# An attention kernel's DMA queue in source order, shift rows two heads at a time, an earlier PSUM release, and one bank for each output half at the end

## The chip, the cores and the metric

The kernel runs on one core of one Trainium2 chip. The metric is the device time of one execution in microseconds (us), as the median of several runs. A core has five engines that run their own instruction streams and meet at semaphores: TensorE (PE, matmuls, with its weight loads shown as PEld), VectorE (DVE), ScalarE (ACT), GpSimd (POOL) and SyncE (SP), which here issues every DMA.

## The reference

One layer of a bidirectional encoder, run on a prompt of 1024 tokens and a sample of 2048 tokens with the same weights. Per layer and sequence:

```python
h = rms_norm(x, norm_pre)
z = h @ w_in        # split into u_pool, g_pool, q, k, v, g_attn, q_x, g_x
pool_out = multiscale_pool(u_pool) * silu(g_pool)
attn_out = block_self_attention(rope(rms_norm(q)), rope(rms_norm(k)), v) * silu(g_attn)   # 8 heads, 2 kv heads
x_out = memory_attention(q_x, k_m, v_m) * silu(g_x)      # 4 heads, 256 memory tokens
mix = concatenate([pool_out, attn_out, x_out])           # 1024 wide
y = mix @ w_out
return x + rms_norm(y, norm_post)
```

Everything is float32 in and out.

## The kernel before

**Two phases.** The first computes the projections, block by block, and puts q, k, v, the gates and the pooled channels into DRAM scratch. The second, which the change is about, does attention, the output projection and the final norm. It is written by hand as a list of *turns* (172 of them), and the loop at L954 to L981 emits one turn after another.

**Pairs, groups and turns.** A `Pair` is 256 query tokens; there are 8 pairs of the sample (s=1), then 4 of the prompt (s=0). Each pair has three `Group`s: kind 0 and kind 1 are the two kv heads of the self-attention (four query heads each), kind 2 is the memory attention. A group's keys come in chunks of 128, two chunks a turn, so a group of kind 0 or 1 takes 8 turns for the sample and 4 for the prompt, and a group of kind 2 one turn. The first pair runs kinds 2, 0, 1 (turns 0; 1 to 8; 9 to 16), every other pair 0, 2, 1.

**What a turn does.** Two *looks* (L171, `largest`): score matmuls into the PSUM tile `N` and a DVE reduction that takes the largest score of each query (L191); they work ahead for a group that comes later. When a group's last look is done, `shift` (L195) transposes the maxima on DVE (L127) and eight small DMAs lay them out as two rows of the tile `rows0` or `rows1` (L206). `weights` (L209) starts a chunk's scores in a PSUM tile `S` with a matmul that adds those rows (L216), adds the scores (L224), and ACT takes the exponential into an SBUF tile `P` (L226; five buffers). `sums` (L228) adds up the `P`s into `z`: for the sample one half of the columns on POOL (L238) and the other on DVE (L239), for the prompt all on DVE. `values` (L241) multiplies by V on PE (L251), each turn or every second turn.

**After a group.** `totals` (L255) sums `z` across partitions on PE, into the PSUM tile `acc`, or into `py` for kind 2 and for the first pair (L260). `take`, `turned` and `inverse` gate the result, transpose the totals, invert them, and send them through a DRAM scratch to be spread over 64 partitions: one DMA out (L280, `rows<-gz`) and two back (L283, `gz<-rows`; `gz` has one buffer). `mix_out` multiplies gate and inverse (L293) and splits the product in a high and a low part (L296, L300), on POOL except for the last pair.

**Output.** `Output.piece` (L366) does the output projection of 128 tokens in two halves of 512 columns, eight chunks of three matmuls each (L381 to L383), into the one PSUM bank `py`; for the last pair both halves share one tile `S` of two banks (`self.both`). `square` (L384) takes the sum of squares on ACT (L388), `scale` (L391) multiplies by the gain on DVE and so ends the use of the bank (L400), `norm` and `out` finish on POOL, ACT and DVE and store (L418). `project` (L934) hands out pieces in the turns without `values`: 4 pieces a turn in the sample, 8 in the prompt.

**What sets the order.** `at(turn, f)` files a step under a time such as turn + 1.4; `due` runs what is filed. Inside a turn the times are: loads and `.0`, first look, `.1`, `sums`, `.2`, weights, second look, `sums`, `.4`, `project`, `values` and `totals`, `.6`. PE, ACT, DVE and POOL follow this order in their streams, since the engines in the set `order` (L508) are under the manual schedule. SP is not in the set: its DMAs are placed by a scheduler that plays the program through with estimated times. On every engine the instructions run in stream order, so a DMA that waits for a semaphore on SP holds up all DMAs behind it.

**Loads at the start of the second phase.** `w_out` comes in eight chunks of 512 KB (L114, `raw<-w_out`), one every two turns, into two buffers; each is split by ACT and POOL in two steps (L118, L119), one a turn, in turns 3 to 18. K and V of a group are loaded when they are first asked for: V from `load_late`, the two other parts of K (DH, DL) from `shift`.

Of the kernel before, what the change touches and what calls it, by code (L numbers as in the profile page):

```python
# [7 lines left out]
F32 = mybir.dt.float32  # L8
# [15 lines left out]
def encoder(ctx, tc, I, O):  # L24
# [63 lines left out]
    has_K, has_V = set(), set()  # L88
# [13 lines left out]
    def load_V(s, kind):  # L102
        has_V.add((s, kind))
# [28 lines left out]
    class Group:  # L132
# [62 lines left out]
        def shift(self):  # L195

            if self.parts > 1:
                nc.vector.tensor_reduce(out=self.top[:, 0:8], in_=self.nb.rearrange("p a i -> p i a"),
                                        axis=AX.X, op=ALU.min)
                load_K(self.s, self.kind, DH, 1)  # L200
                load_K(self.s, self.kind, DL, 2)
            r = lanes_to_rows(self.top, "top")
            for j in range(2):
                row = self.rows[64 * j:64 * j + 1].rearrange("o (i b r) -> o i b r", b=4, r=32)
                for b in range(4):
                    nc.sync.dma_start(out=row[:, :, b].bitcast(F32), in_=r[32 * b + 4 * j:32 * b + 4 * j + 4])  # L206
# [65 lines left out]
        def inverse(self):  # L272
# [6 lines left out]
            rows = dram.tile([4, 256], F32, name="rows", tag="rows", bufs=4)  # L279
            nc.sync.dma_start(out=rows, in_=back[0:128:32])  # L280
            for j in range(2):
                src = rows[2 * j:2 * j + 2].rearrange("l q -> (l q)").unsqueeze(0)
# [65 lines left out]
    class Output:  # L348


        def __init__(self, pair, x):
            self.pair, self.x, self.last = pair, x, pair.last
            self.s, self.t = pair.s, 2 * pair.p + x
            self.both = None
# [11 lines left out]
        def piece(self, h, c, first, final):  # L366
            if self.last:
                if self.both is None:
                    self.start()
                    self.ss = dbl.tile([128, 2], F32, name="ssy", tag="ssy")  # L370
                    self.both = pss.tile([128, 1024], F32, name="S", tag="S")
                ps = self.both[:, 512 * h:512 * h + 512]
            else:
                if first:
                    if h == 0:
                        self.ss = dbl.tile([128, 2], F32, name="ssy", tag="ssy")
                    self.ps = pso.tile([128, 512], F32, name="py", tag="py")
                ps = self.ps
# [6 lines left out]
        def square(self, h):  # L385
            junk = own.tile([128, 512], mybir.dt.bfloat16, name="junk2", tag="junk2")
            src = self.both[:, 512 * h:512 * h + 512] if self.last else self.ps
            nc.scalar.activation(out=junk, in_=src, func=AF.Square, scale=D ** -0.5,  # L388
                                 accum_out=self.ss[:, h:h + 1])

        def scale(self, h):  # L391
            if h == 0 and not self.last:
                for m in sorted(later):
                    for x in [x for x in later[m] if x[0].__name__ in ("norm", "out")]:
                        later[m].remove(x)
                        x[0](*x[1])
                self.start()
            c = slice(512 * h, 512 * h + 512)
            src = self.both[:, c] if self.last else self.ps
            nc.vector.tensor_tensor(out=self.y[:, c], in0=src, in1=npost[:, c], op=ALU.mult)  # L400
# [8 lines left out]
        def out(self, h):  # L409
            s, t, x, y = self.s, self.t, self.xr, self.y  # L410
# [4 lines left out]
            else:  # L415
                nc.scalar.activation(out=y[:, c], in_=y[:, c], func=AF.Copy, scale=self.r[:, 0:1])
                nc.gpsimd.tensor_tensor(out=x[:, c], in0=x[:, c], in1=y[:, c], op=ALU.add)  # L417
            nc.sync.dma_start(out=O[("y_prompt", "y_sample")[s]][0, 128 * t:128 * t + 128, c],  # L418
                              in_=x[:, c])
# [36 lines left out]
    for pair in pairs:  # L456
# [5 lines left out]
        for g in pair.groups:  # L462
            wait = first[g] + g.chunks // 2 + (2 if pair.last else 3)
            at(wait + 0.6, g.mix_out, wait + 1, pair)
        at(max(ends) + (3 if pair.last else 7), open_fill, pair)
    value_runs, sums_at = {}, {}
    for g in groups:
# [4 lines left out]
        while k < c:  # L472
            run = 1 if n + k < first[pairs[1].groups[0]] + 6 else 2
# [550 lines left out]
```

## Time and profile before

| what | us |
|---|---|
| median of 3 runs | 1768.66 |
| lowest and highest run | 1767.05, 1769.37 |
| the profiled execution, its own time | 1766.64 |
| span of the trace in it | 1764.8 |
| of the span, PE busy | 1701.8 |
| DVE busy | 1102.5 |
| POOL busy | 840.2 |
| ACT busy | 657.0 |

In the trace the times count from the start of the span. The first phase ends on PE at about 710, the turns of the sample run to about 1490, those of the prompt to about 1710, and the output projection of the last two pairs ends the kernel. A PE that counts as busy may run at half its clock; the granted clock is shown beside it.

### The profile page before, as it was taken

The page shows a single profiled execution, that of the slowest core. Times are in us where ns is not written, and L with a number is a line of the kernel's source. Part 1 is how long each engine was busy: PE and PEld are TensorE (multiplying, and loading weights), DVE is VectorE, ACT ScalarE, POOL GpSimd, SP SyncE. Part 2 cuts the span into 40 slices and gives each one's busy share as a digit, 9 for nine tenths or more (in the row PEclk, how much of TensorE's full clock was granted, in tenths as well). Part 3 has the DMA queues.
Part 4 walks back from the last instruction along what each step waited for, and adds up shares of the span by engine and source line. Part 5 has one row for each costly group of instructions (what it writes and reads, how often), then busy time and mean ns, then how long its engine had stood idle before and what let it go on. Part 6 is the DMA issues. An engine that isn't in the chain of part 4 may idle for free. (4 is left out here: it accounts for less than half of the span.)

```text
span 1764.8 us, 25545 instructions
## 1 busy us (share of the span) xinstructions
PE 1701.8 (96%) x9400; PEld 1170.4 (66%) x9400; DVE 1102.5 (62%) x1434; ACT 657.0 (37%) x978; POOL 840.2 (48%) x778
## 2 busy tenths in 40 slices
PE   6899999999999999889999999999999999999997
PEld 6889889798898886434555555555555555556565
DVE  6754316551264415679777777777777767877762
ACT  5542225332252211435344444444343443443341
POOL 4556205570054600489556575657665672332231
PEclk9999999999999999989999999999999999999999
DMA  7543634345443392721112121211112341232221
GB/s 253 176 129 108 167 102 140 108 118 143 128 110 119 100 236 52 200 72 55 55 43 90 43 85 49 84 43 56 54 48 84 94 128 57 94 108 74 73 95 66
DMA packets 152716, 178.28 MB, mean 101 GB/s; under 512 B 21760, under 2 KB 121232, under 8 KB 152592
## 3 DMA queue, kind: packets, MB, share of 16 engines
q1 hardware_dynamic: 152592, 176.66, 33.7%
q8 instruction: 74, 1.21, 0.3%
q14 instruction: 50, 0.41, 0.1%
HBM read 121.26 MB, written 55.20 MB: 100 GB/s over the span
## 5 line engine op out<-in xcount | busy, mean ns | idle before, releaser
L191 DVE TENSOR_REDUCE nb<-N 128x2 f32<-128x1024 f32 x320 | 390.9, 1222 | 243.3 <-PE N L186 242.7
L226 ACT ACTIVATE P<-S 128x1024 f32<-128x1024 f32 x344 | 334.7, 1023 | 452.5 <-PE S L224 196.9
L238 POOL TENSOR_TENSOR z<-z,P 128x512 f32<-128x512 f32 x224 | 319.3, 1425 | 162.4 <-ACT P L226 142.5
L251 PE MATMUL acc<-P,V 128*64 128x512 f32 (+1 forms) x1472 | 321.5, 576 | 6.7 <-ACT P L226 2.8
L239 DVE TENSOR_TENSOR z<-z,P 128x512 f32<-128x512 f32 (+1 forms) x272 | 260.5, 958 | 5.5 <-ACT P L226 5.4
L590 PE MATMUL pz<-hT_hi,w_hi 128*128 128x512 f32 x592 | 235.8, 398 | 2.8 <-ACT w_hi L68 1.6
L591 PE MATMUL pz<-hT_lo,w_hi 128*128 128x512 f32 x592 | 233.5, 394 | 0.0
L592 PE MATMUL pz<-hT_hi,w_lo 128*128 128x512 f32 x592 | 231.9, 392 | 0.0
L251 PEld LDWEIGHTS acc<-P,V 128*64 128x64 f32 x1472 | 95.3, 137 | 175.9 <-issue 132.0
L224 PE MATMUL S<-q,DH 64*128 64x512 f32 x1280 | 205.8, 394 | 0.0
L63 POOL TENSOR_TENSOR rs<-rs,mhalf 128x4 f32<-128x4 f32 (+2 forms) x76 | 83.9, 1106 | 211.5 <-DVE rs L61 208.4
L186 PE MATMUL N<-KH,q 64*128 64x512 f32 x640 | 158.2, 486 | 4.4 <-DVE nb L191 3.3
L186 PEld LDWEIGHTS N<-KH,q 64*128 64x128 f32 x640 | 61.1, 183 | 144.5 <-DVE nb L191 63.7
L381 PE MATMUL py<-wo_hi,mix 128*128 128x512 f32 x352 | 145.4, 413 | 2.8 <-DVE y L400 2.8
L590 PE MATMUL pz<-w_hi,hT_hi 128*128 128x384 f32 (+1 forms) x416 | 140.9, 340 | 3.9 <-ACT hT_hi L68 3.9
L591 PE MATMUL pz<-w_lo,hT_hi 128*128 128x384 f32 (+1 forms) x416 | 140.0, 337 | 1.2 <-DVE w_lo L69 1.0
L592 PE MATMUL pz<-w_hi,hT_lo 128*128 128x384 f32 (+1 forms) x416 | 139.9, 337 | 0.0
L224 PEld LDWEIGHTS S<-q,DH 64*128 64x128 f32 x1280 | 122.7, 186 | 23.1 <-issue 2.4
L383 PE MATMUL py<-wo_hi,mix 128*128 128x512 f32 x352 | 137.6, 391 | 0.0
L382 PE MATMUL py<-wo_lo,mix 128*128 128x512 f32 x352 | 137.6, 391 | 0.0
L69 DVE TENSOR_TENSOR w_lo<-wraw,w_hi 128x3072 fp32r<-128x3072 f32 (+2 forms) x21 | 67.8, 3229 | 107.1 <-ACT w_hi L68 106.7
L590 PEld LDWEIGHTS pz<-hT_hi,w_hi 128*128 128x128 f32 x592 | 111.5, 188 | 30.2 <-issue 4.5
(131 smaller groups left out, 2423.3 us busy)
## 6 DMA issues: line engine op xcount, KB each, us to landing
wraw<-w_in SPq DMA_DIRECT2D x15, 1536.0 KB
dg<-gst SPq DMA_DIRECT2D x48, 256.0 KB
q<-dq SPq DMA_DIRECT2D x24, 512.0 KB
gz<-rows SPq DMA_DIRECT2D x72, 128.0 KB
x<-x_sample SPq DMA_DIRECT2D x16, 512.0 KB
xr<-x_sample SPq DMA_DIRECT2D x16, 512.0 KB
y_sample<-xr SPq DMA_DIRECT2D x32, 256.0 KB
dq<-qst SPq DMA_DIRECT2D x96, 64.0 KB
```

What stands on the lines that cost most here:

```text
L186: nc.tensor.matmul(S[:, 512 * j:512 * j + 512], lhsT=self.q[h, 0, 128 * lane:128 * lane + 128], rhs=KH[self.kind][h, 512 * a:512 * a + 512 ...
L191: nc.vector.tensor_reduce(out=out, in_=S, axis=AX.X, op=ALU.max, negate=True)
L224: nc.tensor.matmul(S[:, at + x:at + x + w], lhsT=K, rhs=self.q[h, qx, x:x + w], start=False, stop=n == 2, skip_group_check=True)
L226: nc.scalar.activation(out=self.P[k].rearrange("p j q -> p (j q)"), in_=S, func=AF.Exp)
L238: nc.gpsimd.tensor_tensor(out=z[:, :cut], in0=a[:, :cut], in1=P[:, :cut], op=ALU.add)
L239: nc.vector.tensor_tensor(out=z[:, cut:], in0=a[:, cut:], in1=P[:, cut:], op=ALU.add)
L251: nc.tensor.matmul(self.acc[64 * j:64 * j + 64, x], lhsT=v, rhs=P[:, j, x], start=(k, i) == (0, 0), stop=k == self.chunks - 1, skip_group_ ...
L381: nc.tensor.matmul(ps, lhsT=mh, rhs=wo_hi[:, c, cols], start=first, stop=False)
L382: nc.tensor.matmul(ps, lhsT=mh, rhs=wo_lo[:, c, cols], start=False, stop=False)
L590: nc.tensor.matmul(ps, lhsT=sh, rhs=mh, start=c == 0, stop=False)
L591: nc.tensor.matmul(ps, lhsT=sh, rhs=ml, start=False, stop=False)
L592: nc.tensor.matmul(ps, lhsT=sl, rhs=mh, start=False, stop=c == n - 1)
```

## The change

- SP joins the manual schedule: its DMAs of the second phase stand in the order in which the source emits them. For that order the loads and stores get their own steps: K and V loads are filed with `at` (V of kind 2 first), `inverse` is cut in two (`spread` issues the two DMAs back about half a turn later), and a store follows its `out` by 0.8 turns.
- `shift` writes the rows of both heads with one DMA, so four DMAs take the place of eight.
- The `w_out` chunks come every 2.5 turns instead of every 2; their splits end in turn 21 instead of 18. In the first pair `mix_out` of kinds 2 and 0 is filed three turns later. `values` of kind 2 in the first pair moves from turn 0 to turn 1, and those of turn 1 to turn 2.
- `scale` is filed at turn + 1.1 instead of turn + 1.4, that is ahead of both `sums` steps and the second look of that turn.
- At the end each half of an output has a bank of its own. Once the looks are over, second halves go to the `N` banks that the looks leave free; the four halves of the last pair go to `S`, `N`, `S` and `py`.

What is computed is the same, and so is the number of instructions on PE, ACT, DVE and POOL. SP issues 144 fewer DMAs.

```diff
     def load(self):
             load_K(s, kind, KH, 0)
+            if (s, kind) == (1, 0):
+                load_K(s, kind, DH, 1)
+                load_K(s, kind, DL, 2)
...
         def load_late(self):
-            if (s, kind) not in has_V:
-                load_V(s, kind)
...
             if self.parts > 1:
-                load_K(self.s, self.kind, DH, 1)
-                load_K(self.s, self.kind, DL, 2)
             r = lanes_to_rows(self.top, "top")
-            for j in range(2):
-                row = self.rows[64 * j:64 * j + 1].rearrange("o (i b r) -> o i b r", b=4, r=32)
-                for b in range(4):
-                    nc.sync.dma_start(out=row[:, :, b].bitcast(F32), in_=r[32 * b + 4 * j:32 * b + 4 * j + 4])
+            both = self.rows[0:128:64].rearrange("j (i b r) -> j i b r", b=4, r=32)
+            for b in range(4):
+                nc.sync.dma_start(out=both[:, :, b].bitcast(F32), in_=r[32 * b:32 * b + 8])
...
-            nc.sync.dma_start(out=rows, in_=back[0:128:32])
+            nc.sync.dma_start(out=self.inv, in_=back[0:128:32])
+
+        def spread(self):
             for j in range(2):
...
-        def piece(self, h, c, first, final):
-            if self.last:
-                if self.both is None:
-                    self.start()
-                    self.ss = dbl.tile([128, 2], F32, name="ssy", tag="ssy")
-                    self.both = pss.tile([128, 1024], F32, name="S", tag="S")
-                ps = self.both[:, 512 * h:512 * h + 512]
+        def piece(self, h, c, first, final, end):
...
+                bank = ("S", "N", "S", "py")[2 * self.x + h] if self.last else "N" if end and h else "py"
...
+            if after is None:
+                self.store(h)
+            else:
+                at(after, self.store, h)
...
             wait = first[g] + g.chunks // 2 + (2 if pair.last else 3)
+            if pair is pairs[0] and g.kind != 1:
+                wait += 3
...
-            run = 1 if n + k < first[pairs[1].groups[0]] + 6 else 2
+            run = 1 if 2 < n + k < first[pairs[1].groups[0]] + 6 else 2
...
-        at(n + c + (1.4 if g.kind < 2 else 2.1 if g in pairs[-1].groups else 2.6), g.inverse)
+        if g in pairs[-1].groups:
+            at(n + c + (1.4 if g.kind < 2 else 2.1), g.inverse)
+            at(n + c + (1.4 if g.kind < 2 else 2.1), g.spread)
+        else:
+            at(n + c + (1.4 if g.kind < 2 else 2.6), g.inverse)
+            at(n + c + (2.1 if g.kind < 2 else 3.1), g.spread)
     for c in range(NC):
-        at(2 + 2 * c, load_w_out, c)
+        at(int(2.5 * c + 1), load_w_out, c)
         for h in range(2):
-            at(3 + 2 * c + h + 0.4, split_w_out, c, h)
-    at(4 + 2 * NC, load_npost)
+            at(int(2.5 * c + 1.25 * h + 3) + 0.4, split_w_out, c, h)
+    at(21, load_npost)
+    for s in (1, 0):
+        b = first[pairs[0 if s else 8].groups[0]]
+        at(b - 1 if s == 0 else 0, load_V, s, 2)
+        at(b - 2 if s == 0 else 0.4, load_V, s, 0)
+        at(b + 2.4, load_V, s, 1)
...
     order = {mybir.EngineType.PE, mybir.EngineType.Activation, mybir.EngineType.DVE,
-             mybir.EngineType.Pool}
+             mybir.EngineType.Pool, mybir.EngineType.SP}
...
-                    at(turn + 1.4, out.scale, h)
+                    at(turn + 1.1, out.scale, h)
...
-                        at(turn + (0.6 if out.last else 2.4 + x), out.out, x)
+                        if out.last:
+                            at(turn + 0.6, out.out, x, None)
+                        else:
+                            at(turn + 2.4 + x, out.out, x, None if end else turn + 3.2 + x)
```

**SP in the first pair, about turns 4 to 10.** Each row is one or more DMAs, written out<-in; `rows_5599` is the tile `rows0` and `rows_5600` the tile `rows1`, `rows<-gz` and `gz<-rows` are the inverses on their way out and back, `raw` the chunks of `w_out`, `pg` and `pu` the pooled channels. Before:

```order
L122 DMA npost<-norm_post 128x1024
L167 DMA gate<-dg_0_3_83 128x2x128 x2
L280 DMA rows<-gz 4x256
L283 DMA gz<-rows 64x512 x2
L114 DMA raw<-w_out 128x1024 x2
L321 DMA pg<-dg_0_0_80 128x2x128 x2
L206 DMA rows_5599<-rows_6632 1x4x32 x8
```

and now:

```order
L277 DMA rows<-gz 4x256
L99 DMA DL_6283<-dk_114 64x1024 x4
L282 DMA gz<-rows 64x512 x2
L153 DMA q<-dq_1_0_77 128x1024
L320 DMA pg<-dg_0_0_80 128x2x128 x2
L321 DMA pu<-dp_112 128x2x256
L113 DMA raw<-w_out 128x1024
L203 DMA rows_5599<-rows_6625 2x4x32 x4
```

Before, the rows of the group that starts in turn 9 stood behind two `raw` loads and two `pg` loads of the next pair, all of which wait for POOL to free a buffer; now one `raw` load stands ahead of them, and it waits for a split filed in turn 4.

**DVE in turn 26, where the first `totals` into `py` after a projection follows.** `nb<-N` are the looks' reductions, `rz`, `gz` the transposes and the inverse of the group before. Before:

```order
L191 TENSOR_REDUCE nb<-N 128x2 x2
L270 STREAM_TRANSPOSE rz<-acc 128x256
L239 TENSOR_TENSOR z<-P 128x512
L191 TENSOR_REDUCE nb<-N 128x2
L275 RECIPROCAL rz<-rz 128x8
L278 STREAM_TRANSPOSE gz<-rz 128x256
L400 TENSOR_TENSOR y<-py,npost 128x512
```

and now:

```order
L191 TENSOR_REDUCE nb<-N 128x2 x2
L267 STREAM_TRANSPOSE rz<-acc 128x256
L398 TENSOR_TENSOR y<-py,npost 128x512
L236 TENSOR_TENSOR z<-P 128x512
L191 TENSOR_REDUCE nb<-N 128x2
L272 RECIPROCAL rz<-rz 128x8
L275 STREAM_TRANSPOSE gz<-rz 128x256
```

The read of `py` has moved ahead of four DVE instructions. The same move is made at every output half of the turns.

**SP in a pair of the middle (the third of the sample), around its shift rows.** Before:

```order
L206 DMA rows_5600<-rows_8100 1x4x32 x8
L418 DMA y_sample<-xr 128x512
L151 DMA q<-dq_3_1_87 128x1024
L164 DMA gate<-dg_1_1_90 128x512
L206 DMA rows_5599<-rows_8161 1x4x32 x8
L418 DMA y_sample<-xr 128x512
```

and now:

```order
L203 DMA rows_5600<-rows_8072 2x4x32 x4
L423 DMA y_sample<-xr 128x512
L203 DMA rows_5599<-rows_8129 2x4x32 x4
L167 DMA gate<-dg_1_3_92 128x2x128 x2
L423 DMA y_sample<-xr 128x512
L361 DMA xr<-x_sample 128x1024
```

A store, which waits for POOL, stands between the two sets of rows in both; the q and gate loads that stood there have moved.

More of the change, by code (lines that the diff above doesn't have):

```diff
@@ L102, in load_V @@
     def load_V(s, kind):
-        has_V.add((s, kind))
         if kind == 2:
@@ L364, in start @@
             self.y = dbl.tile([128, D], F32, name="y", **tag)
-        def piece(self, h, c, first, final):
-            if self.last:
-                if self.both is None:
-                    self.start()
-                    self.ss = dbl.tile([128, 2], F32, name="ssy", tag="ssy")
-                    self.both = pss.tile([128, 1024], F32, name="S", tag="S")
-                ps = self.both[:, 512 * h:512 * h + 512]
-            else:
-                if first:
-                    if h == 0:
-                        self.ss = dbl.tile([128, 2], F32, name="ssy", tag="ssy")
-                    self.ps = pso.tile([128, 512], F32, name="py", tag="py")
-                ps = self.ps
+        def piece(self, h, c, first, final, end):
+            if first:
+                if h == 0:
+                    if self.last:
+                        self.start()
+                    self.ss = dbl.tile([128, 2], F32, name="ssy", tag="ssy")
+                bank = ("S", "N", "S", "py")[2 * self.x + h] if self.last else "N" if end and h else "py"
+                if bank == "py":
+                    self.ps[h] = pso.tile([128, 512], F32, name="py", tag="py")
+                else:
+                    ps = (pss if bank == "S" else psn).tile([128, 1024], F32, name=bank, tag=bank)
+                    self.ps[h] = ps[:, 0:512]
+            ps = self.ps[h]
             mh, ml = [m[:, c, self.x] for m in self.pair.mix]
@@ L386, in square @@
             junk = own.tile([128, 512], mybir.dt.bfloat16, name="junk2", tag="junk2")
-            src = self.both[:, 512 * h:512 * h + 512] if self.last else self.ps
-            nc.scalar.activation(out=junk, in_=src, func=AF.Square, scale=D ** -0.5,
+            nc.scalar.activation(out=junk, in_=self.ps[h], func=AF.Square, scale=D ** -0.5,
                                  accum_out=self.ss[:, h:h + 1])
@@ L393, in scale @@
                 for m in sorted(later):
-                    for x in [x for x in later[m] if x[0].__name__ in ("norm", "out")]:
+                    for x in [x for x in later[m] if x[0].__name__ in ("norm", "out", "store")]:
                         later[m].remove(x)
-                        x[0](*x[1])
+                        f, args = x
+                        f(*((args[0], None) if f.__name__ == "out" else args))
                 self.start()
             c = slice(512 * h, 512 * h + 512)
-            src = self.both[:, c] if self.last else self.ps
-            nc.vector.tensor_tensor(out=self.y[:, c], in0=src, in1=npost[:, c], op=ALU.mult)
+            nc.vector.tensor_tensor(out=self.y[:, c], in0=self.ps[h], in1=npost[:, c], op=ALU.mult)
         def norm(self):
@@ L407, in norm, with out @@
             nc.gpsimd.tensor_tensor(out=self.r, in0=s1, in1=mhalf[:, 0:1], op=ALU.pow)
-        def out(self, h):
-            s, t, x, y = self.s, self.t, self.xr, self.y
+        def out(self, h, after):
+            x, y = self.xr, self.y
             c = slice(512 * h, 512 * h + 512)
@@ L417, in out, with store @@
                 nc.gpsimd.tensor_tensor(out=x[:, c], in0=x[:, c], in1=y[:, c], op=ALU.add)
+            if after is None:
+                self.store(h)
+            else:
+                at(after, self.store, h)
+        def store(self, h):
+            s, t, c = self.s, self.t, slice(512 * h, 512 * h + 512)
             nc.sync.dma_start(out=O[("y_prompt", "y_sample")[s]][0, 128 * t:128 * t + 128, c],
-                              in_=x[:, c])
+                              in_=self.xr[:, c])
     CUT = (0, 512)
@@ L939, in project @@
             out, h, c, start, final = fill.pop(0)
-            out.piece(h, c, start, final)
+            out.piece(h, c, start, final, turn >= looked)
             if final:
```

15 lines of the change are left out of this document (11 added, 4 removed).

## Prediction

> **What bounds the kernel now.** I read the page first: which engine is busy all the time, and where it is not.
>
> ```profile
> PE 1701.8 (96%) x9400; PEld 1170.4 (66%) x9400; DVE 1102.5 (62%) x1434; ACT 657.0 (37%) x978; POOL 840.2 (48%) x778
> PE   6899999999999999889999999999999999999997
> PEclk9999999999999999989999999999999999999999
> ```
>
> PE is busy in 1701.8 of 1764.8 us, so no change that leaves the matmuls alone can win more than the 63 us in which it idles, and what it loses to a slow clock. Three places stand out: the first two slices, which are in the projection phase and keep their order, slices 17 and 18, where also the clock drops, and the last slice. Slices 17 and 18 (about 710 to 830) are the first 23 turns. I took that stage apart by windows, with columns PE, PEld, DVE, ACT, POOL, granted clock, DMA share, GB/s:
>
> ```profile
> 711.50:832.20 120.70, 106.18 (x612) 47.87 (x609) 93.73 (x104) 54.03 (x64) 91.11 (x63) 0.94 0.38 114
> 740.50:771.80 31.30, 22.82 (x110) 10.08 (x108) 16.25 (x19) 9.99 (x12) 23.44 (x17) 0.78 0.27 84
> 771.80:832.20 60.40, 57.03 (x332) 24.93 (x328) 55.93 (x61) 30.79 (x37) 54.55 (x37) 1.00 0.16 53
> ```
>
> Of 120.7 us PE idles 14.5, 8.5 of it between 740.5 and 771.8, where the mean clock is 0.78. The next view is who waited for whom, in the stage (first five rows) and on PE from 835 to the end (last four):
>
> ```profile
> POOL gate L293 <- issue: 8.0, 1, 8.0
> PE S L216 <- DMA rows<-rows: 6.2, 3, 4.0
> ACT P L226 <- POOL z L238: 13.3, 5, 4.6
> PE acc L251 <- ACT P L226: 2.8, 1, 2.8
> PE acc L251 <- DMA V<-dvm: 2.6, 1, 2.6
> ...
> PE py L260 <- DVE y L400: 6.9, 8, 1.2
> PE S L381 <- DVE y L400: 4.4, 2, 2.9
> PE py L381 <- DVE y L400: 2.8, 3, 1.6
> PE S L216 <- DMA rows<-rows: 0.4, 2, 0.3
> ```
>
> In the stage three waits of PE end last: for V of the memory attention (2.6), for a `P` that POOL had not freed (2.8), and for shift rows (6.2). From 835 on nearly all that is left is PE waiting for DVE to read a PSUM bank: 6.9 at the `totals`, 2.8 + 4.4 in the last 50 us.
>
> **Part 1, SP's order and the first pair.** The queue of SP shows where the stage's stalls come from:
>
> ```profile
> 740.51 1.10 SPq L283 DMA_DIRECT2D gz<-rows  x2
> 741.70 13.01 SPq L114 DMA_DIRECT2D raw<-w_out  x2
> 756.04 0.89 SPq L321 DMA_DIRECT2D pg<-dg  x2
> 757.03 5.04 SPq L206 DMA_DIRECT2D rows<-rows  x8
> ...
> 744.53 1.28 POOL L293 TENSOR_TENSOR gate<-gate,gz 128x512 f32<-128x512 f32 x1 [8.03 <-issue]
> ...
> 760.88 0.76 PE L216 MATMUL S<-rows,ones_r 64*128 64x512 f32 x1 [4.02 <-DMA rows<-rows]
> 763.23 0.76 PE L216 MATMUL S<-rows,ones_r 64*128 64x512 f32 x1 [1.59 <-DMA rows<-rows]
> ```
>
> SP brings the inverse back at 740.5, POOL stands 8.0 us idle at its multiply until 744.5, meanwhile the `P`s fill up and PE stops for 2.8. Then two `w_out` loads sit at the head of SP for 13.0 us, because POOL, now late, has not freed their buffers; the rows, whose maxima are ready by then, go out only at 757, eight issues in 5.0 us, and PE stops for 4.0 + 1.6. One late transfer made the other.
>
> In the new order the multiply is filed three turns later, the rows have one `w_out` load ahead of them that needs a split from turn 4, and they take four issues instead of eight (by the row above 0.63 each, so 2.5 us instead of 5.0; that a DMA of two rows costs SP more is bounded by nothing and by twice that, which would only restore the 5.0). V of kind 2 is asked for a turn later than now, so its 2.6 goes too. What is moved ahead of the rows are loads of DH, DL and V1, 2.5 MB, that stood ahead of them before as well.
>
> With all these waits gone the stage loses the 14.5 us of idle PE and what the half clock cost. Mean 0.78 over 31.3 us is 13.8 us at half clock; 5.6 of it were idle, the rest costs half, about 4. So PE alone would need 120.7 - 14.5 - 4 = 102.2, a gain of **18.5**. But POOL and DVE worked 91.1 and 93.7 us in this stage, and nothing of that goes. What happens when they are the limit is seen later in it:
>
> ```profile
> 727.69 1.94 ACT L226 ACTIVATE P<-S 128x1024 f32<-128x1024 f32 x2 [2.32 <-PE S L224]
> 731.93 1.94 ACT L226 ACTIVATE P<-S 128x1024 f32<-128x1024 f32 x2 [1.79 <-PE S L224]
> ...
> 790.12 1.27 POOL L119 TENSOR_TENSOR wo_lo<-raw,wo_hi 128x512 fp32r<-128x512 f32 x1
> 791.36 3.47 POOL L238 TENSOR_TENSOR z<-z,P 128x512 f32<-128x512 f32 x2
> 794.79 1.27 POOL L119 TENSOR_TENSOR wo_lo<-raw,wo_hi 128x512 fp32r<-128x512 f32 x1
> ```
>
> A turn that PE sets takes 4.24 (731.93 - 727.69). At 790 three POOL operations a turn, two adds and a split, follow each other without a gap and take 4.67, or 1.56 each. By the code turns 3 to 20 hold 34 adds, 16 splits and 6 multiplies and subtractions of the mix on POOL: 56 x 1.56 = 87.4 if POOL never rests. Turns 0 to 2 took 16.2 (711.5 to 727.7), less 2.6 for V; turns 21 and 22 take 2 x 4.24. Together 109.5, a gain of 11.2. The `w_out` splits are spread over 18 turns instead of 16, which is no relief as long as POOL has no rest. I take **12**, close to the POOL bound, since five buffers of `P` let POOL run only about two turns late.
>
> The Trainium skill, "SBUF — State Buffer", section "Who interferes with whom", says that a DVE instruction with two SBUF inputs and a GpSimd instruction that reads SBUF take one shared port by an exclusive lock, for the whole instruction. The row bears it out in direction: the adds beside DVE take 1.73 (3.47 / 2), the split beside none 1.27. In size it does not: three times 1.27 and two DVE adds of 0.65 (the row of `z<-P` in the next fence) would make 5.1, and the turn took 4.67. What the stage would take by it at full length is the second rival's first case below.
>
> **Part 2, the earlier read of `py`.** Around the third pair's memory attention:
>
> ```profile
> 1040.73 1.23 DVE L191 TENSOR_REDUCE nb<-N 128x2 f32<-128x1024 f32 x1 [2.52 <-PE N L186]
> 1042.24 0.65 DVE L239 TENSOR_TENSOR z<-P 128x512 f32<-128x512 f32 x1
> 1044.74 0.65 DVE L400 TENSOR_TENSOR y<-py,npost 128x512 f32<-128x512 f32 x1
> ...
> 1045.54 0.64 PE L260 MATMUL py<-z,ones 128*32 128x256 f32 x8 [0.76 <-DVE y L400]
> ```
>
> `totals` needs the bank that DVE reads at 1044.74. In the new place, behind the transpose at the first reduction, the read starts near 1042.3 and ends 2.4 us earlier, while PE waits 0.76. So the wait goes whole, at all eight sites: **6.9**. The cost is 0.65 us by which two of DVE's adds and its second reduction start later; DVE waited 2.52 ahead of the first reduction of this very turn, and only a delay of over that would reach PE's next look. Bounds: 0 to 6.9 won; I take 6.9. The two short waits for rows after 835 give 0.4, as the rows are out 2.5 us earlier.
>
> **Part 3, the end.** The banks take away the three waits for `py` at the start of a half, **2.8**. Behind them comes the last pair, where the last two chunks of all four halves are done one half after another:
>
> ```profile
> 1749.04 0.70 ACT junk L388 x2
> 1750.51 0.51 PE S L381
> 1752.21 0.70 ACT junk L388 x2
> 1755.77 0.61 DVE y L400
> 1756.42 0.50 PE S L381
> 1758.84 0.04 DVE y L400
> 1761.07 0.67 DVEq L1020
> ```
>
> These are from the chain of waits that ended last. Now PE starts each second half only when DVE has read the first (1750.51, 1756.42), though the columns differ. With banks of their own, the four halves end 1.38 apart (six matmuls of 0.23 in that chain). Then DVE sets the end: from the second half's square (1752.21) to the end of the third half's scale (1756.38) its work takes 4.17 as before; the fourth half's scale, the norm and the two last outputs follow at once, from 1758.84 to the span's end at 1764.8, 5.96. The second square starts at 1749.04 + 1.38, so the end is 1749.04 + 1.38 + 4.17 + 5.96 = 1760.55, a gain of **4.2**. If DVE were held up by the new order the gain is 0 here and the 2.8 stays. The loads of x for the last pair now stand behind a store of the pair before; they have some 15 us until they are used.
>
> **Sum.** 12 + 6.9 + 0.4 + 2.8 + 4.2 = 26.3. The profiled execution took 1766.64; it becomes 1740.3. The median of the runs shown is 2.0 higher than that execution, so I predict **1742.4**.
>
> **The rivals.** First, *PE's pace*: POOL has enough slack through the five `P`s, and the whole 18.5 is won: 32.8 in all, 1735.9. For it speaks that in 771.8:832.2 PE idles only 3.4 of 60.4 with POOL at 54.55; against it that some of POOL's work there is what the stalls before left over. Second, *the start stays heavy*: POOL's operations and DVE's adds hold each other up at full length, so that turns 3 to 20 take 56 x 1.27 + 34 x 0.65 = 93.2 (the rows of the split and of `z<-P`) and with 13.6 and 8.5 for the other turns 115.3 in all, 5.4 won, 1749.0; or one of SP's old waits simply moves to another load, 0 won, 1754.4. For it speaks the 13.0 us row: a `w_out` load in front of SP waits for POOL as before, and the later splits of turns 14 to 20 fall together with the multiplies of the mix; against it that rows and inverse now have a turn or more between order and use. Third, *no change*: the removed waits at `totals` come back as waits of ACT for a `P`, POOL holds the start at its old length, and only the 2.8 at the end are won: 1765.9. Against it, from 835 to 1490:
>
> ```profile
> ACT P L226 <- POOL z L238: 105.7, 34, 4.3
> ```
>
> So much of such waiting stands there already, and PE does not stop for it.
>
> Fourth, *slower*: in source order a store that waits for POOL's add stands between the two sets of rows of each pair. If POOL is late there, SP parks as it did at 741.70, and PE idles 4.0 + 1.6 as at 760.88. In eleven pairs that is 62 us, less 26.3, so 1804; it decides from 26.3 / 11 = 2.4 us a pair on. Against it: a store is filed 0.8 turns after its `out`, and rows have more than a turn, over 5 us, until they are needed.
>
> **How the numbers follow.** Forecast 0.48 (its own range 1737 to 1747), PE's pace 0.17, heavy start 0.20, no change 0.07, slower 0.08. A measurement of this kernel can tell about 0.2%, 3.5 us. The first three are faster, 0.85. The range holds these three with the bounds of the start, 18.5 and 0: 1733 to 1756; the two left out have 0.15.
>
> **What would show it.** Right: in the stage from 711 no wait of PE for rows or V, a granted clock of 1.0, turns of 4.3 to 4.7, the stage near 109 instead of 120.7; no row "PE py L260 <- DVE y"; the chain at the end without a wait of PE for DVE's scale. Wrong: SP rows of 5 us and more at stores or `w_out` loads with rows behind them, a new wait of PE for rows in every pair, or PE waiting for `P` in turns 14 to 20.

## The result, and the profile after

| | before | changed |
|---|---|---|
| median of the runs, us | 1767.86 (4 runs) | 1746.63 (4 runs) |
| lowest and highest, us | 1766.56, 1769.37 | 1742.98, 1747.99 |
| profiled execution, us | 1766.64 | 1745.43 |
| its span, us | 1764.8 | 1743.6 |

The ratio is 0.9876 with a 95% interval of 0.9858 to 0.9895: 1.2% faster. The forecast was 1742.4 in a range of 1733 to 1756, so the time lies 4.2 us above it and inside. In the spans 21.2 us are gone where the forecast's terms add up to 26.3. Three executions far outside all others are left out of the ratios: one of the kernel before (2750.2 us) and one in each of two experiments (2754.9 and 5772.4).

In the page of the changed kernel the dip in PE's slices 17 and 18 and that of its clock are gone:

```profile
PE 1697.3 (97%) x9400; PEld 1168.0 (67%) x9400; DVE 1116.8 (64%) x1434; ACT 656.7 (38%) x978; POOL 844.3 (48%) x778
PE   7899999999999999999999999999999999999998
PEclk9999999999999999999999999999999999999999
```

By windows (columns as in the prediction), turns 0 to 22 take 106.90 where they took 120.70, at a clock of 1.00 where it was 0.94, and the stretch from the last exponential to the end takes 50.90:

```profile
710.60:817.50 106.90, 100.43 (x610) 45.31 (x610) 97.61 (x104) 53.84 (x65) 91.18 (x61) 1.00 0.41 123
...
1692.70:1743.60 50.90, 43.50 (x198) 32.77 (x194) 17.50 (x30) 11.47 (x24) 7.43 (x8) 0.97 0.30 104
```

The waits of PE from 710 to the end (total us, times, longest):

```profile
PE N L186 <- DVE nb L191: 11.0, 16, 2.2
PE acc L257 <- POOL z L235: 1.1, 4, 0.6
```

Every wait of PE that the prediction quoted is gone: for V, for `P`, for shift rows, for `py`, and at the end. One kind has grown from 3.3 to 11.0: a look (L186) that waits until DVE has read the `N` before it.

To compare kernels stage by stage, I take the start of each turn's first exponential on ACT as its mark. Turns 0 to 22 are the start, 28 to 129 the middle of the sample, 130 to 137 the change to the prompt (the last sample turns), 138 to 170 the prompt, and the tail runs from the exponential of turn 171 to the end. Us from the traces:

| kernel | turn 0 at | 0–22 | 23–27 | 28–129 | 130–137 | 138–170 | tail | span |
|---|---|---|---|---|---|---|---|---|
| before | 711.5 | 120.7 | 28.9 | 575.9 | 45.0 | 224.2 | 58.6 | 1764.8 |
| changed | 710.6 | 106.8 | 28.8 | 572.4 | 48.5 | 225.6 | 50.9 | 1743.6 |
| e1_read_late | 709.8 | 106.9 | 29.6 | 574.2 | 46.4 | 224.2 | 50.9 | 1741.9 |
| e2_prompt_late | 713.0 | 106.9 | 28.7 | 572.2 | 48.5 | 225.0 | 50.9 | 1745.2 |
| e3_keys_later | 709.9 | 106.9 | 28.7 | 572.3 | 45.1 | 225.6 | 50.9 | 1739.4 |
| e11_both | 712.7 | 106.9 | 28.7 | 572.2 | 45.1 | 224.9 | 50.9 | 1741.6 |
| e12_turns_keys | 711.7 | 106.8 | 28.7 | 572.3 | 45.1 | 224.2 | 50.9 | 1739.8 |
| e4b_sp_planned | 709.8 | 106.9 | 28.7 | 572.2 | 45.1 | 225.7 | 50.9 | 1739.3 |
| e5_eight_rows | 711.0 | 109.4 | 28.8 | 572.1 | 49.5 | 226.4 | 51.0 | 1748.2 |
| e6_mix_early | 707.7 | 112.3 | 28.7 | 572.4 | 49.6 | 225.7 | 50.9 | 1747.3 |
| e7_wout_two | 713.4 | 107.3 | 28.3 | 572.4 | 47.7 | 225.6 | 50.9 | 1745.7 |
| e9_values_tail | 712.0 | 106.8 | 28.8 | 572.4 | 46.3 | 225.6 | 59.0 | 1750.9 |
| e10_no_split | 711.9 | 103.3 | 28.3 | 572.3 | 46.5 | 225.7 | 50.9 | 1738.8 |

The first phase, whose order the change leaves alone, ends anywhere between 707.7 and 713.4. Behind it, stages that an edit doesn't touch repeat within 0.1 us, all but 130 to 137. So small effects are read from the stages, since a median of a few runs carries part of the first phase's scatter too. The -0.9 of the first phase below lies inside it.

From before to changed the stages moved by -0.9 (first phase), -13.8, -0.1, -3.5, +3.5, +1.3 and -7.7: -21.2.

### The profile page after: what moved, and what is told of

It reads as the page before. It is cut to its first block, busy times and chain, and to the rows that moved or that the text cites. A ratio compares the mean times of both kernels' runs of the same rounds, so it can differ in the third digit from the quotient of the medians.

```text
span 1743.6 us, 25303 instructions
## 1 busy us (share of the span) xinstructions
PE 1697.3 (97%) x9400; PEld 1168.0 (67%) x9400; DVE 1116.8 (64%) x1434; ACT 656.7 (38%) x978; POOL 844.3 (48%) x778
## 5 line engine op out<-in xcount | busy, mean ns | idle before, releaser
L235 POOL TENSOR_TENSOR z<-z,P 128x512 f32<-128x512 f32 x224 | 324.2, 1447 | 160.2 <-ACT P L223 140.4
L236 DVE TENSOR_TENSOR z<-z,P 128x512 f32<-128x512 f32 (+1 forms) x272 | 269.3, 990 | 4.5 <-ACT P L223 4.3
L221 PE MATMUL S<-q,DH 64*128 64x512 f32 x1280 | 201.6, 392 | 0.0
L186 PE MATMUL N<-KH,q 64*128 64x512 f32 x640 | 157.0, 487 | 12.4 <-DVE nb L191 11.0
L186 PEld LDWEIGHTS N<-KH,q 64*128 64x128 f32 x640 | 59.8, 183 | 153.2 <-DVE nb L191 86.4
L380 PE MATMUL py<-wo_hi,mix 128*128 128x512 f32 x336 | 139.0, 414 | 0.0
L69 DVE TENSOR_TENSOR w_lo<-wraw,w_hi 128x3072 fp32r<-128x3072 f32 (+2 forms) x21 | 67.8, 3227 | 107.3 <-ACT w_hi L68 106.9
L382 PE MATMUL py<-wo_hi,mix 128*128 128x512 f32 x336 | 131.6, 392 | 0.1
L381 PE MATMUL py<-wo_lo,mix 128*128 128x512 f32 x336 | 131.5, 391 | 0.0
```

Source lines behind the costliest of these rows:

```text
L186: nc.tensor.matmul(S[:, 512 * j:512 * j + 512], lhsT=self.q[h, 0, 128 * lane:128 * lane + 128], rhs=KH[self.kind][h, 512 * a:512 * a + 512 ...
L221: nc.tensor.matmul(S[:, at + x:at + x + w], lhsT=K, rhs=self.q[h, qx, x:x + w], start=False, stop=n == 2, skip_group_check=True)
L235: nc.gpsimd.tensor_tensor(out=z[:, :cut], in0=a[:, :cut], in1=P[:, :cut], op=ALU.add)
L236: nc.vector.tensor_tensor(out=z[:, cut:], in0=a[:, cut:], in1=P[:, cut:], op=ALU.add)
L380: nc.tensor.matmul(ps, lhsT=mh, rhs=wo_hi[:, c, cols], start=first, stop=False)
L382: nc.tensor.matmul(ps, lhsT=ml, rhs=wo_hi[:, c, cols], start=False, stop=final)
```

## The experiments

All start from the changed kernel.

**The change to the prompt: +3.5.** In the timeline of the changed kernel (start, duration, then the engine's idle time and what ended it):

```profile
1409.24 1.44 SPq L99 DMA_DIRECT2D DH<-dk  x2
1410.72 1.46 SPq L99 DMA_DIRECT2D DL<-dk  x2
1412.28 0.56 SPq L277 DMA_DIRECT2D rows<-gz  x1
1419.79 1.10 SPq L282 DMA_DIRECT2D gz<-rows  x2
...
1423.30 1.27 POOL L292 TENSOR_TENSOR gate<-gate,gz 128x512 f32<-128x512 f32 x1 [1.79 <-DMA gz<-rows]
...
1424.61 0.45 DVE L275 STREAM_TRANSPOSE gz<-rz 128x256 f32<-128x256 f32 x1 [4.14 <-POOL gate L292]
1424.97 1.19 DVE L191 TENSOR_REDUCE nb<-N 128x2 f32<-128x1024 f32 x1
...
1426.22 0.66 PE L186 MATMUL N<-KH,q 64*128 64x512 f32 x2 [2.24 <-DVE nb L191]
```

From the bottom up: PE waits 2.24 for a reduction, which stands on DVE behind the next group's transpose into `gz`, which waits 4.14 for POOL to have read the one buffer of `gz`; POOL waits for the inverse, and the inverse's way back is issued only at 1419.79, 7.5 us after its way out at 1412.28. The prompt's keys had been issued just ahead of it. `e3_keys_later` moves them:

```diff
-                at(b - 8 + 0.2, load_K, s, 0, (None, DH, DL)[a], a)
+                at(b - 8 + 3.2, load_K, s, 0, (None, DH, DL)[a], a)
```

> The loads of the prompt's DH and DL of kind 0 are filed 3 turns later (five turns ahead of their use), behind the inverses of the last sample pair's kinds 0 and 2. Theory: these 1 MB stood ahead of the 4 KB of the inverse in the DMA engines (busy 0.95 to 1.04 from 1409 to 1418), the inverse came 6.0 us late, POOL multiplied late, DVE's transpose waited 4.1 behind it and PE 2.24 plus about 1.3 at half clock. Then the stretch of eight turns goes from 48.5 to about 45, 3.5 us won, no wait of over 0.5 us of PE there. Rival: the inverse is late because its way back is now issued half a turn later; then the stretch stays at 48.5 within 0.5.

It took 1742.19 us (0.9864, 0.9849 to 0.9880). The stage is 45.1, and its timeline reads:

```profile
1409.44 0.56 SPq L277 DMA_DIRECT2D rows<-gz  x1
1413.32 1.10 SPq L282 DMA_DIRECT2D gz<-rows  x2
...
1420.69 1.28 POOL L292 TENSOR_TENSOR gate<-gate,gz 128x512 f32<-128x512 f32 x1
1422.00 0.45 DVE L275 STREAM_TRANSPOSE gz<-rz 128x256 f32<-128x256 f32 x1 [2.31 <-POOL gate L292]
```

From the inverse's way out to its way back it is now 3.9 us instead of 7.5, and POOL finds the inverse there. The Trainium skill, "DMA: Bandwidth & Descriptors", section "Queues, rings and completion order", says that each DMA engine takes the descriptors of a ring in order; a 4 KB transfer that comes late behind 1 MB of keys agrees with it. The rival is out. In the kernels that keep the keys first, the stage scatters between 46.3 and 49.6; in the four that don't, it is 45.1. So the place of the keys costs between 1.2 and 4.5 us; the 3.5 is what it cost in this one profile.

**The early read of `py`.** `e1_read_late` files it as before:

```diff
-                    at(turn + 1.1, out.scale, h)
+                    at(turn + 1.4, out.scale, h)
```

> The changed kernel with the read of py filed at turn + 1.4 again; all else stays. By the forecast's term the eight waits return whole: 6.9 us slower than the changed kernel, wherever they stood. By the theory after the two traces the early read is worth 3.5 us in the middle of the sample (575.9 to 572.4 between the same turns) and costs 1.4 in the prompt (224.2 to 225.6), so this kernel is about 2 to 3 us slower in all: middle of the sample near 576, six waits of PE at the totals of about 0.76 again, prompt near 224 with two waits of 1.17 and fewer waits of the looks for DVE. If the time of the early read only moved to other waits, it is the same within 1 us.

It took 1745.05 (0.9882, 0.9864 to 0.9900), no slower at all. The forecast's 6.9 is out. By stages the late read costs 0.8 in turns 23 to 27 and 1.8 in 28 to 129, and wins 1.4 in the prompt; the 2.1 between 130 and 137 lies inside that stage's scatter. So the early read is worth 2.6 - 1.4 = 1.2 us net. In the third pair of the changed kernel `py` is read 2.35 us ahead of `totals`, about as forecast, and PE does not wait there; but at the `totals` into `acc` ahead of it PE now waits for POOL's part of `z`:

```profile
1024.68 0.64 PE L257 MATMUL acc<-z,ones 128*32 128x256 f32 x8 [0.19 <-POOL z L235]
...
1027.30 0.65 DVE L398 TENSOR_TENSOR y<-py,npost 128x512 f32<-128x512 f32 x1
...
1029.65 0.64 PE L257 MATMUL py<-z,ones 128*32 128x256 f32 x8
```

In e1_read_late the same instruction waits:

```profile
1030.58 0.64 PE L257 MATMUL py<-z,ones 128*32 128x256 f32 x8 [0.76 <-DVE y L398]
```

Of 0.76, 0.48 is left as a shorter pair (95.65 us instead of 96.13); 0.19 has gone to the wait for `z`. In the prompt the sign turns. DVE there adds whole `P` tiles, 1.2 us each, and what is put ahead of a reduction makes a look late. One prompt pair of the changed kernel:

```profile
1534.89 0.69 DVE L398 TENSOR_TENSOR y<-py,npost 128x512 f32<-128x512 f32 x1 [1.09 <-POOL xr L415]
...
1549.77 0.65 DVE L398 TENSOR_TENSOR y<-py,npost 128x512 f32<-128x512 f32 x1
1550.34 1.20 DVE L236 TENSOR_TENSOR z<-P 128x1024 f32<-128x1024 f32 x1
1551.47 1.22 DVE L191 TENSOR_REDUCE nb<-N 128x2 f32<-128x1024 f32 x1
...
1554.26 1.21 DVE L191 TENSOR_REDUCE nb<-N 128x2 f32<-128x1024 f32 x1
...
1538.37 0.51 PE L186 MATMUL N<-KH,q 64*128 64x512 f32 x2 [0.43 <-DVE nb L191]
...
1541.06 0.49 PE L186 MATMUL N<-KH,q 64*128 64x512 f32 x2 [0.30 <-DVE nb L191]
...
1555.52 0.50 PE L186 MATMUL N<-KH,q 64*128 64x512 f32 x2 [0.89 <-DVE nb L191]
```

The wait of 1.18 at `totals` is gone, and three waits at looks stand in its place: 0.43 + 0.30 + 0.89 = 1.62. `e2_prompt_late` reads late for the outputs of the prompt, and `e11_both` adds the move of the keys:

```diff
-                    at(turn + 1.1, out.scale, h)
+                    at(turn + (1.1 if out.s else 1.4), out.scale, h)
```

> The read of py at turn + 1.4 in the prompt alone, at turn + 1.1 in the sample. Theory: in the prompt DVE adds whole P tiles (1.2 us) and is the busier engine, so the early read pushes the reductions of the looks back by more than the wait of 1.17 it saves; the prompt (225.6 us between the same two turns) goes back to 224.2, 1.4 us won, the waits of the looks for DVE there (0.43, 0.30, 0.89 a pair) go and two of 1.17 at the totals come. Rival: the prompt's added 1.4 comes from the order of SP or from the stores, then 225.6 stays or grows by 2.3.

> Both: read of py late in the prompt alone, and the prompt's DH and DL loaded three turns later. If the two are separate, 1.4 + 3.5 = 4.9 us faster than the changed kernel, about 1741.7 as a median beside 1746.6. If one of the two only moves a wait, the other's share alone.

They took 1745.60 (0.9870 to 0.9901) and 1742.65 (0.9852 to 0.9883). The prompt fell only to 225.0 and 224.9, 0.6 instead of 1.4, so both expectations were missed in size. The reason was in the code: the output of the last sample pair is projected in the prompt's turns too, and kept its early read. `e12_turns_keys` asks for the turn's sequence instead:

```diff
-                    at(turn + 1.1, out.scale, h)
+                    at(turn + (1.1 if turns[turn][0].s else 1.4), out.scale, h)
```

> The prompt's DH and DL loaded three turns later, and py read at turn + 1.4 in the prompt's turns (so for the last sample pair's output too, which is projected there), at turn + 1.1 in the sample's. If the stages add up as the runs so far show, the eight turns at the change of sequence take 45.1, the prompt 224.2, all else is as in the changed kernel: 4.8 us below it, a median of 1741.8 at the changed kernel's 1746.6, or 1740.5 to 1743 with the first phase's scatter. If the late read alone gave the prompt its 224.2 only together with a late read in the sample, the prompt stays at 225.

It took 1741.07 (0.9854, 0.9837 to 0.9870), with 45.1 and 224.2 in the two stages: they add up. It beats the kernel before. Its four executions (1740.6 to 1741.9) all lie below the four of the changed kernel (1743.0 to 1748.0) and its stages behind the first phase are 4.9 shorter, but the two intervals of the ratio overlap; nor does its interval part it from e3_keys_later.

**The start: which part cured it.** `e4_sp_planned` takes SyncE out of the hand order and leaves all else; the streams of the other engines are the same row by row.

```diff
     order = {mybir.EngineType.PE, mybir.EngineType.Activation, mybir.EngineType.DVE,
-             mybir.EngineType.Pool, mybir.EngineType.SP}
+             mybir.EngineType.Pool}
```

> SyncE is taken out of the hand order again; everything else of the change stays, and the orders of PE, ACT, DVE and POOL are those of the changed kernel. The planner puts the first rows of the first pair behind two loads of w_out and two of the next pair's channels again. Theory, order of SP: the start (turns 0 to 22, 106.8 us in the changed kernel, 120.7 before) goes back by most of the 13.9, to 115 to 121, with PE waiting for rows. Rival, the new filing of loads and multiplies alone brings it: the start stays at 107 within 1 us. The middle of the sample (572.4) stays within 1 us by the first, since SP has time there.

> SyncE out of the hand order again, for a profile at full clock (the first one fell in a run of 2754.9 us at a clock of 0.57). That kernel took 1743.2 as a median, 3.4 less than the changed one. Theory: the start is as in the changed kernel within 1 us, so the source order is not what cures it, and the 3.4 is the stall at the change of sequence, where the planner lets the inverse go ahead of the prompt's keys (45 instead of 48.5 in those eight turns). Rival: the start is 3 us shorter still and the stall is there.

Three executions took 1742.2 to 1743.6 (ratio 0.9868, 0.9851 to 0.9886), and the one of e4b_sp_planned, the same kernel, 1741.03. The start is 106.9, the same as in the changed kernel: the first expectation, which was also the forecast's reason, fell. The whole kernel is even 3.4 us faster than the changed one by the medians, and in the profile of e4b_sp_planned turns 130 to 137 take 45.1 instead of 48.5, because the planner lets the inverse go ahead of the prompt's keys. SP's timeline at the start:

```profile
733.59 0.56 SPq L277 DMA_DIRECT2D rows<-gz  x1
738.31 1.10 SPq L282 DMA_DIRECT2D gz<-rows  x2
739.50 3.53 SPq L113 DMA_DIRECT2D raw<-w_out  x2
743.92 0.89 SPq L320 DMA_DIRECT2D pg<-dg  x2
746.09 2.29 SPq L203 DMA_DIRECT2D rows<-rows  x4
```

In the changed kernel:

```profile
732.06 1.18 SPq L282 DMA_DIRECT2D gz<-rows  x2
...
747.01 2.29 SPq L203 DMA_DIRECT2D rows<-rows  x4
```

Counted from turn 0, the inverse goes back at 28.5 (738.31 - 709.8) instead of 21.5 (732.06 - 710.6), and the rows stand behind two `raw` loads again; yet they leave at 36.3, as in the changed kernel (36.4). POOL does not stop for the inverse, because its multiply is filed three turns later, so the `raw` buffers come free in time and the rows are not held up. `e6_mix_early` undoes that filing:

```diff
             if pair is pairs[0] and g.kind != 1:
-                wait += 3
+                wait += 0
```

> In the first pair the multiplies of kinds 2 and 0 are filed three turns earlier, as before. By the forecast the inverse comes late for POOL, and PE stops for P: 2.8 us or more longer in turns 0 to 22. By the trace of the changed kernel the inverse is spread at 732 to 733 and lands near 735, the multiply would be due near 734: POOL idles about 1 us once, the start grows by 0.5 to 1.5 from 106.8. If SP's new order alone cures the start, it stays at 106.8 within 0.4.

1749.61 (0.9901, 0.9876 to 0.9926). Even in source order:

```profile
734.82 1.29 POOL L292 TENSOR_TENSOR gate<-gate,gz 128x512 f32<-128x512 f32 x1 [3.55 <-DMA gz<-rows]
...
755.68 1.08 PE L257 MATMUL py<-z,ones 128*32 128x256 f32 x8 [2.84 <-POOL z L235]
```

and by its windows

```profile
749.40:764.30 14.90, 11.87 (x62) 5.53 (x60) 9.12 (x12) 5.02 (x7) 12.35 (x10) 0.77 0.00 0
```

POOL idles 3.55, PE stops for 2.84 some 20 us later, and the mean clock is 0.77 over the 14.9 us around that stop: 5.5 us in all. The first expectation (2.8 or more) holds, the other two do not, and the chain is the one that the forecast describes: late inverse, POOL, then PE. `e5_eight_rows` sends a DMA for each head again:

```diff
-            both = self.rows[0:128:64].rearrange("j (i b r) -> j i b r", b=4, r=32)
-            for b in range(4):
-                nc.sync.dma_start(out=both[:, :, b].bitcast(F32), in_=r[32 * b:32 * b + 8])
+            for j in range(2):
+                row = self.rows[64 * j:64 * j + 1].rearrange("o (i b r) -> o i b r", b=4, r=32)
+                for b in range(4):
+                    nc.sync.dma_start(out=row[:, :, b].bitcast(F32), in_=r[32 * b + 4 * j:32 * b + 4 * j + 4])
```

> Rows go out one head at a time, eight DMAs of 0.57 instead of four, at the same places in the order of SP. Theory: the rows land 2.3 us later and have more than a turn to spare, so start, sample and prompt stay within 0.5 us each. Rival: the pairs of 96.8 us that the kernel before had beside those of 96.2 came from late rows; then two or more of the sample's pair periods (95.65 now) grow by 0.6 and the prompt grows too, 1 to 4 us in all.

1750.41 (0.9912, 0.9897 to 0.9927), 3.8 above the changed kernel. The start grew by 2.6 and the prompt by 0.8; the sample's pairs stayed. In its timeline:

```profile
747.59 5.09 SPq L204 DMA_DIRECT2D rows<-rows  x8
...
753.82 0.46 PE L214 MATMUL S<-rows,ones_r 64*128 64x512 f32 x1 [0.72 <-DMA rows<-rows]
```

Four DMAs take 2.29 (above), eight 5.09: a DMA of two rows costs SP no more than one of a single row. The rows could start at 747 and are asked for near 753, 6 us later; 5.09 and the way to SBUF are too long for that. At the second group PE waits 0.78, and the two turns with these waits are 1.2 us longer each. The forecast's "over 5 us" until rows are needed was right, but eight DMAs use it up. `e7_wout_two` puts the `w_out` steps back to their old turns:

```diff
-        at(int(2.5 * c + 1), load_w_out, c)
+        at(2 + 2 * c, load_w_out, c)
...
-            at(int(2.5 * c + 1.25 * h + 3) + 0.4, split_w_out, c, h)
+            at(3 + 2 * c + h + 0.4, split_w_out, c, h)
```

> w_out's chunks come every 2 turns and their splits stand in turns 3 to 18, one a turn, as before the change; the rest stays. By the forecast spreading them is no relief: turns 0 to 22 stay at 106.8 within 0.5. By the theory from the run without the splits (4.29 us a turn without one, 4.67 with one, where DVE's second add takes 1.8 instead of 0.7), the number of turns with a split stays 16, so again about 0, except where splits now meet the multiplies of the first pair and the loads meet the rows: up to 3 more.

1747.65 (0.9891, 0.9876 to 0.9906). 0.5 more up to turn 22 and 0.5 less in the five turns after: no relief, as forecast. `e10_no_split` asks what sets the start now. It leaves out POOL's subtractions, and PE multiplies by `wo_hi` in the place of `wo_lo`.

```diff
-        nc.gpsimd.tensor_tensor(out=wo_lo[:, c, x], in0=raw[:, x], in1=wo_hi[:, c, x].bitcast(F32), op=ALU.subtract)
...
-            nc.tensor.matmul(ps, lhsT=mh, rhs=wo_lo[:, c, cols], start=False, stop=False)
+            nc.tensor.matmul(ps, lhsT=mh, rhs=wo_hi[:, c, cols], start=False, stop=False)
```

> The low part of w_out is not computed: POOL's 16 subtractions (1.63 us each in turns 3 to 20) are left out and PE reads the high part in their place, so PE's work is the same. If POOL still sets the start, turns 0 to 22 fall from 106.8 to the pace of PE, 102 to 103. If DVE sets it (77.4 of 82.7 us busy in turns 3 to 20), they stay above 105.5, less only what DVE's adds gain when no split runs beside them.

1741.06 (0.9857, 0.9842 to 0.9872), start 103.3. DVE's groups of turns 3 to 20 in the changed kernel (count, busy us, mean ns), and then in this one:

```profile
L191 DVE TENSOR_REDUCE nb<-N 128x2 f32<-128x1024 f32 x37 | 45.1, 1218 | 5.5 <-PE N L186 5.4
L236 DVE TENSOR_TENSOR z<-z,P 128x512 f32<-128x512 f32 x32 | 32.1, 1002 | 0.0
```

```profile
L190 DVE TENSOR_REDUCE nb<-N 128x2 f32<-128x1024 f32 x37 | 45.2, 1222 | 9.5 <-PE N L185 9.5
L235 DVE TENSOR_TENSOR z<-z,P 128x512 f32<-128x512 f32 x32 | 24.5, 766 | 0.0
```

DVE has the same work in both, but its adds take 1002 ns on average with the splits and 766 without. In a run of turns with splits the first still take about 4.3, while POOL falls behind; turns at the end of a run or right behind it (6 and 7, 12, 20 to 22) take 4.67. Without splits all of these take 4.29. In turn 6 of the changed kernel the only wait of PE is a look's:

```profile
741.84 0.50 PE L186 MATMUL N<-KH,q 64*128 64x512 f32 x2 [0.31 <-DVE nb L191]
```

In turns 0 to 22 such waits for DVE add up to 5.1 us, and to 2.7 without the splits; PE waits there neither for a `P` nor for POOL. By the windows of the changed kernel, turns 3 to 20 and then 21 and 22 (DVE's busy time is the third after the length, POOL's the fifth):

```profile
725.40:808.10 82.70, 78.36 (x460) 33.95 (x458) 77.39 (x85) 42.43 (x51) 76.52 (x51) 1.00 0.35 108
808.10:817.50 9.40, 8.69 (x54) 3.74 (x52) 9.40 (x9) 5.45 (x8) 9.24 (x7) 1.00 0.08 23
```

In the last two DVE is busy for 9.40 of 9.40 and POOL for 9.24. So POOL's splits cost the start 3.5 us, and where PE stops for them, it waits for DVE, whose adds are longer beside them.

**Values in turn 0, and the tail.** `e9_values_tail` undoes two parts, the place of `values` in turns 0 to 2 and the banks of the end:

```diff
-            run = 1 if 2 < n + k < first[pairs[1].groups[0]] + 6 else 2
+            run = 1 if n + k < first[pairs[1].groups[0]] + 6 else 2
...
-                bank = ("S", "N", "S", "py")[2 * self.x + h] if self.last else "N" if end and h else "py"
...
+                if not self.last:
+                    self.ps[h] = pso.tile([128, 512], F32, name="py", tag="py")
+                elif h:
+                    self.ps[1] = self.pt[:, 512:1024]
+                else:
+                    self.pt = pss.tile([128, 1024], F32, name="S", tag="S")
+                    self.ps[0] = self.pt[:, 0:512]
```

> Two parts undone, 900 us apart and read by stage. Start: the values of the memory attention go back to turn 0, those of turn 1 to turn 1, V's load stays first in its order. If V of kind 2 is late as before, PE waits up to 2.6 us in turns 0 to 2 and the start grows by 1.5 to 2.6 from 106.8; if its earlier load is enough, by under 0.5. Tail: both halves of an output share a tile, second halves go to py again. By the forecast the stretch from the last exponential to the end grows from 50.9 by 2.8 + 4.2 to 57.9, with five waits of PE for DVE's read; if only one half of it matters, to 53.7 or 55.1.

1754.53 (0.9930, 0.9916 to 0.9945). At the start PE waits for V again, but nothing is lost:

```profile
714.38 1.95 PE L248 MATMUL acc<-P,V 128*64 128x256 f32 x16 [1.20 <-DMA V<-dvm]
```

Turns 0 to 2 take 14.7 in both kernels, where before took 16.2 with a wait of 2.6. So the 1.4 to 1.5 us come from V of kind 2 being there earlier (the wait is 1.2 instead of 2.6), and the move of `values` brings nothing. The tail takes 59.0, 8.1 more than in the changed kernel, with the old waits:

```profile
PE S L381 <- DVE y L399: 4.4, 2, 2.9
PE py L381 <- DVE y L399: 3.2, 3, 1.6
```

## Why the prediction was right, and where it was not

The sum came near for partly lucky reasons. Start, tail and first phase won 3.4 us more than forecast, the reads of `py` and the change to the prompt 8.5 less, and these errors offset each other in part.

| term | forecast | traces |
|---|---|---|
| start, turns 0 to 22 | -12 | -13.8 |
| reads of `py` and late rows | -7.3 | -2.3 (-3.6 to turn 129, +1.3 in the prompt) |
| tail | -7.0 | -7.7 |
| change to the prompt | 0 | +3.5 |
| first phase | 0 | -0.9 |

**The start: right size, wrong cause.** The 109.5 of a POOL that never rests was too long: I counted 56 POOL operations in turns 3 to 20, while with the later filing 51 fell there, busy for 76.5 of 82.7. That POOL's work lengthens the start is shown: without the splits it goes to 103.3, near the 102.2 of PE alone. But POOL does rest, and what PE waits for is DVE. Wrong was what cures the stalls. I gave it to SP's order first; taken away alone, that order costs nothing here, and gives 3.4 back at the change to the prompt. For V, I gave its 2.6 to the later `values`; the move brought nothing. Taken away alone, the later multiply costs 5.5, the two-head rows 2.6, the spacing of `w_out` 0.5. The earlier load of V is worth 1.4 to 1.5. Added up, that makes about 10 of 13.8. Source order and later multiply may be two cures of one stall, so that either alone hides what the other is worth; both undone together were not tried, and the last 4 us stay open.

**The reads of `py` and the late rows: mis-sized, with the wrong sign in the prompt.** "So the wait goes whole" held at every site. The step that failed is that 0.65 us earlier on DVE would delay nothing that PE waits for: I took DVE's 2.52 of idle time in a turn of the sample and used it for the prompt, where DVE adds twice as many columns. The bound of 0 to 6.9 held; the value should have been worked out for each sequence. Of the 3.5 in turns 28 to 129, 1.8 is the read. Most of the rest stood in two pairs (96.8 us where the others took 96.2), in one turn of each, 0.66 and 0.72 longer than in e1_read_late. These are the turns in which PE waited for rows. In the kernel before, the first of them reads:

```profile
1129.39 1.41 SPq L151 DMA_DIRECT2D q<-dq  x1
...
1137.34 0.49 PE L216 MATMUL S<-rows,ones_r 64*128 64x512 f32 x1 [0.18 <-DMA rows<-rows]
```

The load of q ahead of the rows kept SP for 1.41 us, where it took 0.35 in the pair ahead. In the other pair the eight row DMAs took 5.83 instead of 4.93. So the term of late rows, put at 0.4, was worth about 1.4. These waits are gone both with eight row DMAs in the new order of SP and with four in the planned one, so either of the two is enough beside the rest of the change.

**The change to the prompt: missed.** I asked what stands ahead of the rows in SP's new order, not what stands ahead of the inverse. It is the second rival's mechanism, a load in front of a small transfer, though at another place than I looked.

**The tail: right.** The waits of 7.2 went as worked out; 7.7 were won, and 8.1 come back when the banks are shared again.

**The rivals.** Rows behind the stores never made PE wait: no pair is longer. Full blocking between POOL and DVE would have made the start 115.3; it is 106.8. PE's own pace is what the start reaches only without the splits.

## What to carry to other kernels

Ahead of a small transfer that someone waits for, look for loads that are not needed soon: behind 1 MB of keys the 4 KB took 7.5 us instead of 3.9. When an instruction moves ahead on an engine, work out its price in each stage with that stage's own slack. And where several edits cure one stall, undoing each alone says what it is worth beside the others, not what it would have brought by itself.

## What the runs showed of the hardware that was not expected

Half clock after short stops of PE: in the changed kernel's windows behind the stop of 2.24 us,

```profile
1424.00:1427.00 3.00, 0.78 (x4) 0.39 (x6) 2.40 (x3) 1.32 (x2) 2.92 (x3) 0.90 0.00 1
1427.00:1430.00 3.00, 3.00 (x8) 0.81 (x8) 2.42 (x3) 0.00 (x0) 0.14 (x1) 0.53 0.46 115
```

the granted clock is 0.53 for 3 us, which by an estimate adds 3 x (1 - 0.53) = 1.4 to the stop's 2.24. In e1_read_late a stop of 1.76 at the same place was followed by 1.00:

```profile
1428.50:1432.00 3.50, 3.50 (x20) 1.21 (x18) 2.29 (x3) 0.00 (x0) 0.27 (x2) 1.00 0.59 176
```

The Trainium skill, "TensorE: Matmul & The Clock Gate", section "HAM oscillation — how this bites in real kernels", gives the rule as no idle gaps of PE over about 3.4 us; here 2.24 was enough. In e2_prompt_late, behind a stop of 2.04 at the same place, the granted clock was 0.50 from 1428.9 to 1432.3. Not every such stop does it: the one of 2.6 for V in the kernel before, in turn 0, left the clock at 1.00:

```profile
711.50:727.70 16.20, 13.59 (x103) 7.37 (x102) 9.54 (x12) 5.94 (x7) 5.56 (x4) 1.00 0.99 280
```

The stop in e7_wout_two, at the same place as the one of 2.24, lasted 3.10 us, and the clock stayed at 1.00 behind it:

```profile
1429.90:1433.30 3.40, 3.38 (x16) 1.25 (x18) 3.22 (x3) 0.00 (x0) 0.94 (x1) 1.00 0.33 83
```

So in these traces the length of a stop does not decide by itself; what does is not shown.
